# A hybrid layer whose context columns and preparation run within the feed-forward part before it

## The chip, the cores and the metric

The kernel runs on one core of one Trainium2 chip. The metric is the device time of one execution in microseconds (us). TensorE (PE in the profile) multiplies, and its weight loads (PEld) run beside; VectorE (DVE), ScalarE (ACT) and GpSimd (POOL) work element by element; SyncE (SP) issues nearly all DMAs. Each engine takes its instructions in the order written in its own stream, and waits for the others by semaphores.

## The reference

The program is two blocks. The first has layers of feed-forward, mixer, feed-forward on 256 tokens of width 1024; its last part is called FFN(1,1) here. The second works on 256 latent tokens (the output of the first) and 256 context tokens (an input of the program) and begins with the hybrid layer, cut to what matters here:

```
p_lat, p_ctx = norm(h) @ w_in, norm(ctx) @ w_in       # 1792 RWKV columns, then 1536 of attention
rc = rwkv_prepare(p_ctx[:, :1792]);  rl = rwkv_prepare(p_lat[:, :1792])
yc, sf, sb = wkv_bidir(rc, zero state)                # both directions
yl, _, _   = wkv_bidir(rl, (sf, sb))                  # begins from the context's last states
a_lat, a_ctx = rwkv_output(yl, rl), rwkv_output(yc, rc)
o_l = differential attention of latents over latents and context
o_c = differential attention of the context over itself
out = [a, norm(o)] @ w_out                            # for latents and context
```

The context's half, `p_ctx` and `rc`, needs nothing of the first block. `yl` needs `sf` and `sb`, so the two `wkv_bidir` are serial.

## The kernel before

Everything is float32. A weight tile is loaded by SP (`wr`, `wload`), cast to a high part by ACT (`wh`) and a low part is subtracted by DVE (`wl`; while `poolw` is 3, every third one by POOL); a product is then three matmuls (`mm3`, lines 135 to 137). A framework takes the order in which the code is written, priorities (`rank`, `beside`) and the life of the buffers in pools, simulates the engines, and from that fixes each engine's stream.

`ffn` runs over eleven tiles j of 256 hidden columns: an up-projection into PSUM banks B, the gate on ACT and DVE, a down-projection into banks A, which are kept over all j. Its argument `side(j)` is called once per j and may insert other work. Before, `side(3)` normalises the context and transposes it (`norm_T`). After FFN(1,1) comes `hybrid`, stage by stage:

- the latents' norm, then seven units of 256 RWKV columns for the context (`cols(0, u)`: 48 matmuls of 256 wide each, 336 in all; `mix` then adds the two neighbours in time);
- `rw_prep` for the context (gates, decays, and a serial triangular inverse on DVE, here called the Neumann loop: 62 operations at L1162), and beside it the attention's columns for both token sets (288 matmuls of 512 wide, `A<-xH,wh` and `A<-wh,xH`);
- the context's attention, `attention(0)`, among the latents' 336 column matmuls (`cols(1, u)`); the latents' mixed columns go to DRAM (`lr`);
- `chains` for the context: eight groups of heads and directions over four chunks, a recurrence in which each hop is a few small matmuls with copies on ACT and DVE between (L1355, L1363, L1368, L1373, L1379, L1389), and whose preparation (`s`, `Z` on POOL, `W`, `sys` on DVE, L1322) can go ahead. Beside it runs `rw_prep` for the latents, from the `lr` read back;
- `chains` for the latents, with `attention(1)` beside it;
- the output projection, then the next part (`mlp2`).

Buffers live in pools on a left and a right side of SBUF that close in order, so a pool's place decides when the next stage's loads may start.

## Time and profile before

| | us |
|---|---|
| median of 3 runs | 3198.22 (3195.32 to 3206.99) |
| profiled execution | 3196.53 |
| its span | 3194.8 |
| FFN(1,1) | 1467 to 1663 |
| latents' norm, context's RWKV columns | 1663 to 1713 |
| `rw_prep` of the context, attention columns | 1713 to 1797.5 |
| `attention(0)`, latents' RWKV columns | 1797.5 to 1858 |
| context's chains, `rw_prep` of the latents | 1858 to 2026 |
| latents' chains, `attention(1)` | 2026 to 2158 |
| output projection | 2158 to 2224 |

The span runs from the first instruction to the last; 1.7 us of the execution lie around it. The stages are read from where the lines of each begin and end on TensorE; the last Neumann operation of the latents falls at 2030.8. The profile's granted clock (PEclk) is TensorE's, in parts of 2.4 GHz: 0.959 over the span. In a row of windows there stand the stretch and its length, then the busy time and, in brackets, the count of instructions of PE, PEld, DVE, ACT and POOL, the granted clock, the DMA engines' busy share and GB/s. A row of a group has line, engine, operation, what is written and read, the count, busy us in all, mean ns of one, and the idle time just before them with what ended it.

### The profile page before, as it was taken

The numbers are of one execution on the slowest core, as the hardware profiler recorded it, in microseconds if no ns is written. First come the engines' busy times: TensorE is split into PE (matmuls) and PEld (weight loads), VectorE is DVE, ScalarE is ACT, GpSimd is POOL, SyncE is SP. The second block draws the span as 40 slices with busy tenths as digits, with TensorE's granted clock in tenths as the row PEclk, the third lists the DMA queues.
The fourth block names the chain that finished last, engine by engine and source line by source line (L and its number), as shares of the span: only waits on it lengthen the run. The fifth ranks groups of instructions, "written<-read, shape, count | busy, mean of one in ns | idle before, by whom it ended". The sixth has DMA issues, their size and how long they took to land.

```text
span 3194.8 us, 42767 instructions
## 1 busy us (share of the span) xinstructions
PE 2955.0 (92%) x15184; PEld 2459.9 (77%) x15184; DVE 2202.2 (69%) x3572; ACT 1589.6 (50%) x2907; POOL 608.2 (19%) x806
## 2 busy tenths in 40 slices
PE   8999989889989998999999978898999989998898
PEld 7877878668778787877887867786777777777787
DVE  6666875676677668657565767886766548999755
ACT  5454544545455454445446575665423325565444
POOL 1221020121221003001012155430110002444100
PEclk9999999899999999999999987898999989999999
DMA  7666655556667654647544611115466424344564
GB/s 248 217 208 179 177 161 171 172 189 209 202 199 224 181 168 131 203 145 244 176 142 146 191 45 41 51 41 191 147 192 190 152 74 114 111 116 126 185 186 139
DMA packets 383577, 509.76 MB, mean 160 GB/s; under 512 B 39938, under 2 KB 245140, under 8 KB 382980
## 3 DMA queue, kind: packets, MB, share of 16 engines
q1 hardware_dynamic: 383364, 507.03, 51.6%
q8 instruction: 120, 1.97, 0.3%
q14 instruction: 93, 0.76, 0.1%
HBM read 494.07 MB, written 12.88 MB: 159 GB/s over the span
## 4 chain that ended last, share of the span: by engine, by line
PE 59%; DVE 17%; DMA 8%; issue 7%; ACT 5%; POOL 3%; SPq 0%; DVEq 0%; ACTq 0%; POOLq 0%
PE A L135 11%; PE A L137 11%; PE A L136 11%; DMA wr<-in_ada_w_dram 5%; PE B L136 5%; PE B L135 5%; PE B L137 5%; DVE wl L253 4%; DVE scv L1476 2%; ACT wh L252 2%; DVE adacc L706 2%; PE T L243 1%; DMA wr<-in_mlp_w_dram 1%; PE F L135 1%; PE F L137 1%
## 5 line engine op out<-in xcount | busy, mean ns | idle before, releaser
L253 DVE TENSOR_TENSOR wl<-wr,wh 128x1024 fp32r<-128x1024 f32 x720 | 902.0, 1258 | 481.8 <-ACT wh L252 448.0
L252 ACT CAST wh<-wr 128x1024 fp32r<-128x1024 f32 x720 | 751.5, 1049 | 712.4 <-PE A L137 320.7
L135 PE MATMUL B<-wh,xH 128*128 128x512 f32 x832 | 330.4, 403 | 7.4 <-ACT xH L252 5.5
L136 PE MATMUL B<-wl,xH 128*128 128x512 f32 x832 | 332.3, 400 | 3.1 <-DVE wl L253 3.0
L137 PE MATMUL B<-wh,xL 128*128 128x512 f32 x832 | 330.2, 397 | 0.0
L135 PE MATMUL A<-xH,wh 128*128 128x256 f32 (+1 forms) x960 | 305.8, 321 | 1.7 <-ACT zm L950 1.0
L706 DVE SCALAR_TENSOR_TENSOR adacc<-wr,silu_c,adacc 128x512 f32<-128x512 f32 x232 | 181.6, 801 | 177.3 <-DMA wr<-in_ada_w_dram 104.5
L136 PE MATMUL A<-xL,wh 128*128 128x256 f32 (+1 forms) x960 | 303.7, 318 | 0.0
L137 PE MATMUL A<-xH,wl 128*128 128x256 f32 (+1 forms) x960 | 298.1, 318 | 1.4 <-DVE wl L253 0.8
L136 PE MATMUL A<-wl,hTH 128*128 128x512 f32 x736 | 285.9, 391 | 3.1 <-DVE wl L253 3.1
L135 PE MATMUL A<-wh,hTH 128*128 128x512 f32 x736 | 282.9, 391 | 4.6 <-ACT hTH L252 3.1
L137 PE MATMUL A<-wh,hTL 128*128 128x512 f32 x736 | 282.0, 392 | 0.1
L136 PE MATMUL A<-wl,xH 128*128 128x512 f32 x544 | 217.6, 400 | 9.2 <-DVE wl L253 6.3
L135 PE MATMUL A<-wh,xH 128*128 128x512 f32 x544 | 215.7, 404 | 4.9 <-ACT xH L255 3.6
L137 PE MATMUL A<-wh,xL 128*128 128x512 f32 x544 | 217.1, 400 | 0.0
L135 PEld LDWEIGHTS A<-xH,wh 128*128 128x128 f32 x960 | 184.3, 192 | 14.2 <-issue 1.9
L137 PEld LDWEIGHTS A<-xH,wl 128*128 128x128 f32 x960 | 181.8, 192 | 14.9 <-issue 1.9
L136 PEld LDWEIGHTS A<-xL,wh 128*128 128x128 f32 x960 | 184.3, 192 | 11.4 <-issue 1.5
L135 PEld LDWEIGHTS B<-wh,xH 128*128 128x128 f32 x832 | 159.1, 192 | 42.5 <-ACT xH L252 7.2
L136 PEld LDWEIGHTS B<-wl,xH 128*128 128x128 f32 x832 | 159.3, 191 | 37.6 <-DVE wl L253 6.5
L137 PEld LDWEIGHTS B<-wh,xL 128*128 128x128 f32 x832 | 159.4, 192 | 33.1 <-DVE xL L253 0.4
L205 POOL TENSOR_TENSOR ms<-ss 128x1 f32<-128x1 f32 x44 | 16.1, 367 | 875.1 <-ACT jk L268 451.0
(530 smaller groups left out, 6153.0 us busy)
## 6 DMA issues: line engine op xcount, KB each, us to landing
wr<-in_w_ffn_gu_dram SPq DMA_DIRECT2D x352, 256.0 KB
wr<-in_w_in_dram SPq DMA_DIRECT2D x144, 512.0 KB
wr<-in_mlp_w_dram SPq DMA_DIRECT2D x128, 512.0 KB
wr<-in_ada_w_dram SPq DMA_DIRECT2D x96, 512.0 KB
wr<-in_w_ffn_down_dram SPq DMA_DIRECT2D x88, 512.0 KB
wr<-in_w_branch_dram SPq DMA_DIRECT2D x48, 512.0 KB
wr<-in_ssd_w_in_dram SPq DMA_DIRECT2D x48, 512.0 KB
wr<-in_hy_w_in_dram SPq DMA_DIRECT2D x40, 512.0 KB
```

Source lines behind the costliest of these rows:

```text
L135: mm(acc, xH, wH, start=start, stop=False)
L136: mm(acc, xH, wL, start=False, stop=False)
L137: mm(acc, xL, wH, start=False, stop=stop)
L205: nc.gpsimd.tensor_tensor(out=m, in0=ss[:, 0:1], in1=ss[:, 1:2], op=ALU.add)
L243: nc.tensor.transpose(pt[:, i * P : (i + 1) * P], src[:, i * P : (i + 1) * P], self.ident)
L252: nc.scalar.copy(H, src)
L253: nc.vector.tensor_tensor(out=L, in0=src, in1=H.bitcast(F32), op=ALU.subtract)
L706: nc.vector.scalar_tensor_tensor(out=a, in0=w[:, k % 2, :], scalar=c, in1=a, op0=ALU.mult, op1=ALU.add)
L1476: nc.vector.scalar_tensor_tensor(out=v3(y), in0=z[:, :, j : j + S], scalar=self.scw(j, f), in1=v3(y), op0=ALU.mult, op1=ALU.add)
```

## The change

- `hybrid_open` is called before FFN(1,1): the hybrid layer's parameters are loaded there.
- `hybrid_ctx` is a generator that `side(j)` steps through, by the table `SIDE` (2, 3, 4, ... steps for each j): context norm, the seven units of columns (now in the order `RWU`, each unit in one PSUM bank F, operands swapped, so that the product comes out transposed), then all of `rw_prep`.
- After FFN(1,1) the layer has three stretches: the context's chains with the latents' RWKV columns stepped among them (one step every two rounds of the chains; `poolw` is 3); then `rw_prep` of the latents and, at the same rank, the attention's columns and after them `attention(0)`; then the latents' chains with `attention(1)`, as before.
- The normalised tokens of both sets go through DRAM (`xs`) to the stretch of the attention's columns; the round trip of `lr` is gone. `rw_prep` runs its large products on DVE alone (before, for the latents some were on POOL).
- Chains' buffers `nch` are 8 in the first stretch and 9 in the last, `s2` 2 or 3 (before 9 and 3). The feed-forward part's last down weights come from the common pool (`own=False`). Sides of pools change (`swap`), and the output projection's inputs `x` are loaded earlier in SP's stream, before the last chains.

```diff
+RWU = (2, 3, 6, 0, 1, 4, 5)
+SIDE = (2, 3, 4, 4, 4, 4, 5, 5, 5, 5, 5, 0)
...
-    def ffn(self, l, i, h, side=None, g_in=None):
+    def ffn(self, l, i, h, side=None, g_in=None, own=True):
...
+    def rw_cols(self, u, xT):
+        nc, pr, W = self.nc, self.pr, self.I["hy_w_in_2"][0]
+        ws = [self.wload([W[q * 512 : q * 512 + 512, u * 256 : u * 256 + 256]], 4) for q in range(2)]
+        ps = self.accTF() if self.two else self.accF()
+        for i in range(2):
+            fs = slice(i * P, i * P + P)
+            for k in range(KT):
+                wh, wl = (a[:, k % 4, fs] for a in ws[k // 4])
+                self.mm3(ps[:, i * S : i * S + S], wh, wl, xT[0][:, k, :], xT[1][:, k, :], k == 0, k == KT - 1)
+            if i == 0:
+                yield 1
...
+    def hybrid_ctx(self):
...
+        for u in RWU:
+            yield from self.rw_cols(u, xT)
+            yield 1
+        self.v0 = self.rv
+        yield from self.rw_prep(self.bgs[0], itertools.repeat(self.accF), nc.vector, nc.vector)
...
-        self.norm_mod(self.lat_mods, [h[:, t, :] for t in range(NT)], xT, 2)
+        xT = tuple(Halves([self.t(self.rwp, (P, 4, S), "tmp", F32R, 4) for _ in range(2)]) for _ in range(2))
+        self.norm_mod(self.lat_mods, [h[:, t, :] for t in range(NT)], xT)
...
-        for u in range(7):
-            cols(0, u)
-        cx = self.rw_prep(pt, pa, rk, v[0], gd[0], bg[0], itertools.cycle((self.accB, self.accB, self.accF)), nc.vector, nc.vector)
-        self.poolw = 3
+        pl, self.nch = self.pool(ec, "rwc", "right"), 8
+        cg = self.chains(pl, self.arrs, self.v0, y[0], None, True)
+        self.poolw = 3
...
+        for n in itertools.count():
+            if next(cg, None) is None:
+                break
+            if n == 1:
+                lg = lat()
+            if n >= 2 and n % 2 == 0:
+                next(lg, None)
...
+        for _ in self.rw_prep(bg[1], itertools.cycle((self.accB, self.accB, self.accF)), nc.vector, nc.vector):
+            pass
         with self.rank(r0):
...
-        for u in range(7):
-            cols(1, u)
-            for _ in range(3):
-                next(dg, None)
+            el.close()
+            for _ in attention(0):
+                pass
+            ed.close()
...
-        for _ in self.chains(pl, cx, v[0], y[0], None, True):
-            pass
-        with self.rank(r0):
-            nc.sync.dma_start(out=rk, in_=lr)
-            lx = self.rw_prep(pt, self.pool(el, "rwl", "right"), rk, v[1], gd[1], bg[1], itertools.repeat(self.accF), nc.vector, nc.gpsimd)
...
         def side(j):
-            if j == 3:
...
+            for _ in range(SIDE[j]):
+                next(cg, None)
-        self.ffn(1, 1, h, side)
+        self.ffn(1, 1, h, side, own=False)
```

How instructions move, at three places. First VectorE's stream at the end of FFN(1,1) of the kernel before (L275 is the residual, L233 and L235 the latents' norm, L253 a split of a weight):

```order
L275 SCALAR_TENSOR_TENSOR h_81<-xn_14642,rs_14651,h_81 128x512
L275 SCALAR_TENSOR_TENSOR h_81<-xn_14646,rs_14651,h_81 128x512
L253 TENSOR_TENSOR wl_14871<-wr_14868,wh_14870 128x1024
L233 SCALAR_TENSOR_TENSOR xn_14673<-h_81,rs_14671,md_13571 128x512
L233 SCALAR_TENSOR_TENSOR xn_14683<-h_81,rs_14671,md_13571 128x512
L235 TENSOR_TENSOR xn_14673<-xn_14673,md_13569 128x512
L253 TENSOR_TENSOR wl_14901<-wr_14898,wh_14900 128x1024
L235 TENSOR_TENSOR xn_14683<-xn_14683,md_13569 128x512
L233 SCALAR_TENSOR_TENSOR xn_14703<-h_81,rs_14701,md_13571 128x512
L233 SCALAR_TENSOR_TENSOR xn_14713<-h_81,rs_14701,md_13571 128x512
```

The same place after (L294 is the residual, L252 and L254 the latents' norm, L1211 on `tmp` the Neumann loop of the context, L272 on `tmp` the low halves of the transposed latents, L1361 the chains' preparation):

```order
L294 SCALAR_TENSOR_TENSOR h_84<-xn_15488,rs_15497,h_84 128x512
L294 SCALAR_TENSOR_TENSOR h_84<-xn_15492,rs_15497,h_84 128x512
L1211 TENSOR_TENSOR tmp_15055<-tmp_15055,tmp_15056 128x31
L1211 TENSOR_TENSOR tmp_15056<-tmp_15054,tmp_15055 128x30x2
L1211 TENSOR_TENSOR tmp_15055<-tmp_15055,tmp_15056 128x30x2
```

```order
L1211 TENSOR_TENSOR tmp_15055<-tmp_15055,tmp_15056 128x2x30
L1211 TENSOR_TENSOR tmp_15056<-tmp_15054,tmp_15055 128x31
L1211 TENSOR_TENSOR tmp_15055<-tmp_15055,tmp_15056 128x31
L272 TENSOR_TENSOR tmp_15507<-F_15522,tmp_15505 128x4x128
L272 TENSOR_TENSOR tmp_15507<-F_15552,tmp_15505 128x4x128
L272 TENSOR_TENSOR tmp_15508<-T_15532,tmp_15506 128x4x128
L1466 COPY vr_15616<-v_13417 128x512
L272 TENSOR_TENSOR tmp_15508<-T_15562,tmp_15506 128x4x128
L1361 TENSOR_TENSOR sys_15608<-B_15603,c_hyb_13004 128x2x128
```

Before, the norm follows the residual at once, and the Neumann loop stands a stage later. Now all 62 of its operations stand between the residual and the four low halves, without which no latent column can be multiplied.

Second TensorE's stream in the context's chains of the kernel before (`F<-ari,bk` is `rw_prep` of the latents, the rest are the chains):

```order
L1389 MATMUL A_17390<-c_all_67,E_17120 128x128
L1379 MATMUL A_17394<-xv_3449_16842,sys_17133 128x64 x2
L1373 MATMUL A_17416<-u_3598_17316,Z_17192 128x128
L1239 MATMUL F_18441<-ari_3908_18314,bk_3910_18316 64x64 x16
L1379 MATMUL A_17420<-xv_3449_16842,sys_17075 128x64 x2
L1379 MATMUL A_17442<-xv_3458_16878,sys_17097 128x64 x2
L1373 MATMUL A_17464<-u_3602_17326,Z_17156 128x128
L1368 MATMUL A_17468<-u_3619_17381,sys_17239 128x128
```

And after (L154 to L156 on F are the latents' columns, L1381, L1382, L1414 and L1469 the chains):

```order
L156 MATMUL F_15737<-tmp_15505,wl_15728 128x256
L154 MATMUL F_15737<-tmp_15505,wh_15727 128x256
L155 MATMUL F_15737<-tmp_15507,wh_15727 128x256
L1414 MATMUL A_15657<-xv_3178_15579,W_15607 128x64 x2
L1469 MATMUL T_15590<-c_all_67,v_13417 128x128 x4
L156 MATMUL F_15737<-tmp_15505,wl_15728 128x256
L154 MATMUL F_15737<-tmp_15505,wh_15727 128x256
L155 MATMUL F_15737<-tmp_15507,wh_15727 128x256
L156 MATMUL F_15737<-tmp_15505,wl_15728 128x256
```

The chains' matmuls now stand in the same stream between runs of 7 to 12 column matmuls; the last column matmul stands where 13 of the chains' 32 hops are done, and the other 19 have only the beginning of `rw_prep` beside them.

Third TensorE's stream at `attention(0)` of the kernel before (L1122, L1134 and L1139 are the attention, L135 to L137 the latents' columns):

```order
L1139 MATMUL F_16305<-dv_16031,dwT_16303 128x128 x2
L1122 MATMUL B_16446<-dk_16030,qz_3290_16114 128x256
L1134 MATMUL T_16329<-c_all_67,dw_16316 128x128 x2
L137 MATMUL A_16686<-xH_12994,wl_16690 128x256
L135 MATMUL A_16686<-xH_12994,wh_16689 128x256
L136 MATMUL A_16686<-xL_12995,wh_16689 128x256
```

And after (L1169, L1181 and L1186 are the attention, L154 to L156 the last of the attention's columns, L1331 the end of `rw_prep`):

```order
L154 MATMUL A_18137<-wh_18230,xH_17850 128x512
L155 MATMUL A_18137<-wl_18231,xH_17850 128x512
L156 MATMUL A_18137<-wh_18230,xL_17851 128x512
L1169 MATMUL B_18289<-dk_18275,qz_3817_18280 128x256
L1169 MATMUL B_18296<-dk_18275,qz_3817_18280 128x256
L1169 MATMUL B_18316<-dk_18275,qz_3817_18280 128x256
L1169 MATMUL B_18323<-dk_18275,qz_3817_18280 128x256
L1181 MATMUL T_18306<-c_all_67,dw_18293 128x128 x2
L1169 MATMUL B_18345<-dk_18275,qz_3818_18281 128x256
L1186 MATMUL F_18311<-dv_18276,dwT_18309 128x128 x2
```

Before, column matmuls stand between the attention's steps. Now the attention stands alone, from the last column matmul to the first matmul of the latents' chains 25 rows on; on VectorE its operations stand behind the latents' Neumann loop, and ahead of the latents' chains.

## Rows read from the trace of the kernel before

**Rows 1.** Page: TensorE's busy share, and the granted clock in 40 slices.

```profile
PE 2955.0 (92%) x15184; PEld 2459.9 (77%) x15184; DVE 2202.2 (69%) x3572; ACT 1589.6 (50%) x2907; POOL 608.2 (19%) x806
...
PEclk9999999899999999999999987898999989999999
```

**Rows 2.** Windows by stage: us, busy (count) by engine, PEclk, DMA share, GB/s.

```profile
1467.00:1663.00 196.00, 193.29 (x871) 157.08 (x872) 116.90 (x154) 90.49 (x133) 6.77 (x19) 0.99 0.54 173
1663.00:1713.00 50.00, 44.43 (x337) 42.60 (x335) 31.53 (x52) 33.25 (x60) 15.02 (x26) 0.93 0.56 171
1713.00:1797.50 84.50, 84.15 (x477) 64.73 (x477) 46.00 (x49) 42.10 (x71) 13.10 (x8) 1.00 0.51 145
1797.50:1858.00 60.50, 55.21 (x425) 52.88 (x424) 57.55 (x166) 40.44 (x113) 12.85 (x16) 1.00 0.54 168
1858.00:2026.00 168.00, 135.00 (x836) 111.01 (x834) 123.28 (x343) 94.84 (x327) 84.05 (x125) 0.78 0.13 39
2026.00:2158.00 132.00, 117.74 (x831) 105.13 (x832) 106.60 (x356) 91.31 (x362) 60.76 (x100) 0.94 0.16 49
2158.00:2224.00 66.00, 56.30 (x223) 42.38 (x224) 42.25 (x62) 35.38 (x46) 2.84 (x6) 0.90 0.54 188
```

**Rows 3.** Windows: context columns (256 wide), feed-forward matmuls (512 wide).

```profile
1689.00:1704.00 15.00, 15.00 (x127) 15.00 (x127) 9.02 (x10) 12.16 (x23) 3.21 (x5) 1.00 0.69 200
1500.00:1600.00 100.00, 99.62 (x452) 81.81 (x451) 57.14 (x70) 45.06 (x58) 0.00 (x0) 1.00 0.61 189
```

**Rows 4.** Groups of VectorE, 1797.5 to 1858: count, busy, mean ns, idle.

```profile
L1162 DVE TENSOR_TENSOR tmp<-tmp,tmp 128x31 f32<-128x31 f32 (+15 forms) x62 | 23.9, 386 | 6.6 <-DMA tmp<-in_id_dram 6.0
L1124 DVE TENSOR_REDUCE dmx<-B 128x1 f32<-128x256 f32 x16 | 6.6, 413 | 0.0
L1131 DVE SCALAR_TENSOR_TENSOR dw<-dw,dmx,dw 128x256 f32<-128x256 f32 x8 | 4.2, 524 | 0.0
L1130 DVE TENSOR_SCALAR dw<-dw,dmx 128x256 f32<-128x256 f32 x8 | 2.7, 342 | 0.0
L1128 DVE RECIPROCAL dmx<-dmx 128x1 f32<-128x1 f32 x16 | 2.5, 156 | 0.3 <-ACT dw L1127 0.2
```

**Rows 5.** Groups of VectorE, 1663 to 1689.

```profile
L233 DVE SCALAR_TENSOR_TENSOR xn<-h,rs,md 128x512 f32<-128x512 f32 x4 | 2.8, 747 | 0.4 <-POOL rs L209 0.4
L235 DVE TENSOR_TENSOR xn<-xn,md 128x512 f32<-128x512 f32 x4 | 2.7, 685 | 0.0
L275 DVE SCALAR_TENSOR_TENSOR h<-xn,rs,h 128x512 f32<-128x512 f32 x3 | 2.2, 749 | 0.1
L253 DVE TENSOR_TENSOR xL<-T,xH 128x512 fp32r<-128x512 f32 x2 | 1.4, 684 | 0.0
```

**Rows 6.** Windows at the start of the context columns.

```profile
1680.00:1685.00 5.00, 2.98 (x13) 2.84 (x14) 1.80 (x10) 1.44 (x4) 0.70 (x2) 0.58 0.29 77
1685.00:1690.00 5.00, 5.00 (x34) 5.00 (x33) 2.36 (x7) 1.99 (x5) 0.57 (x2) 0.74 0.73 209
```

**Rows 7.** Windows: context's chains, latents' chains, first hop to last.

```profile
1880.70:2026.00 145.30, 123.72 (x797) 102.98 (x796) 115.64 (x323) 78.53 (x281) 70.27 (x89) 0.81 0.10 30
2044.20:2158.00 113.80, 106.70 (x787) 96.50 (x787) 93.21 (x317) 75.25 (x308) 48.90 (x80) 0.99 0.10 32
```

**Rows 8.** Groups of TensorE, 2026 to 2158, attention(1) among the chains.

```profile
L1122 PE MATMUL F<-kr,qr 128*128 128x256 f32 x32 | 11.4, 440 | 1.6 <-DVE kr L1112 1.0 <-ACT dw L1127 0.4
L1122 PE MATMUL F<-dk,qz 128*128 128x256 f32 x32 | 10.5, 413 | 0.0
```

**Rows 9.** Chain of waits, 1850 to 1885: start us, us, what.

```profile
1853.69 2.62 DMA db<-tmp
...
1858.59 5.82 DMA rk<-lr
```

**Rows 10.** Chain of waits, 2155 to 2182.

```profile
2157.52 8.38 DMA on<-od
...
2178.25 0.85 PE A L135 x2
```

More of the change, by code (lines that the diff above doesn't have):

```diff
@@ L292, in do_down @@
                 for j in js:
-                    own = dict(pool=p, bufs=(2, 2, 2)) if j == NJ - 1 else {}
-                    ws.append([self.wload([wd[j * 256 : j * 256 + 256, n * 512 : n * 512 + 512]], **own) for n in range(2)])
+                    mine = dict(pool=p, bufs=(2, 2, 2)) if own and j == NJ - 1 else {}
+                    ws.append([self.wload([wd[j * 256 : j * 256 + 256, n * 512 : n * 512 + 512]], **mine) for n in range(2)])
                 for t in range(NT):
@@ new lines, in hybrid_open, with rw_in @@
+        self.bgs = [scr((P, 8, S), f"bg{s}") for s in range(2)]
+        self.rwa, self.rwp = self.pool(self.ea, "rwa", "right"), self.pool(self.et, "rwp", "right")
+        self.hybrid_setup(b)
+    def rw_in(self):
+        b = self.hyb
+        self.rk, self.rv, self.gd = self.t(b, (P, 9, S), "rk"), self.t(b, (P, 4, S), "v"), self.t(b, (P, S), "gd")
+    def rw_cols(self, u, xT):
[9 more added lines that the diff above has]
+                yield 1
+        z = self.t(self.rwp, (P, 2, 514), "kk" if u % 2 else "kb")
+        nc.gpsimd.memset(z[:, :, 0:1], 0.0)
+        nc.gpsimd.memset(z[:, :, S + 1 : S + 2], 0.0)
+        pv = ps.rearrange("p (i s) -> p i s", i=2)
+        nc.scalar.copy(z[:, :, 1 : S + 1], pv)
+        n = z[:, :, S + 2 : 2 * S + 2]
+        nc.gpsimd.tensor_tensor(out=n, in0=z[:, :, 0:S], in1=z[:, :, 2 : S + 2], op=ALU.add)
+        for i in range(2):
+            f = 2 * u + i
+            o = self.rv[:, f - 8, :] if 8 <= f < 12 else self.gd if f == 13 else self.rk[:, min(f, 8), :]
+            nc.scalar.activation(o, pv[:, i, :], AF.Identity, scale=pr["mu1"](f))
+            nc.vector.scalar_tensor_tensor(out=o, in0=n[:, i, :], scalar=pr["mu2"](f), in1=o, op0=ALU.mult, op1=ALU.add)
@@ L923, in hybrid @@
+        xT = tuple(Halves([self.t(self.rwp, (P, 4, S), "tmp", F32R, 4) for _ in range(2)]) for _ in range(2))
+        self.norm_mod(self.lat_mods, [h[:, t, :] for t in range(NT)], xT)
+        for i in range(2):
+            for k in range(0, KT, 4):
+                nc.sync.dma_start(out=self.xs[i][:, k : k + 4, S : 2 * S], in_=xT[i][:, k : k + 4, :].bitcast(F32))
         for e in eh:
             e.close()
-        b = self.pool(eb, "hyb")
-        self.pad(b, 32)
-        self.hybrid_setup(b)
@@ L973, in hybrid @@
         with self.rank(r0):
             DQ = 1792
+            px = self.pool(el, "hyx")
+            xT = self.xT(px, "x", n=2 * S)
+            for k in range(0, KT, 2):
+                for i in range(2):
+                    nc.sync.dma_start(out=xT[i][:, k : k + 2, :].bitcast(F32), in_=self.xs[i][:, k : k + 2, :])
             qks, vds = scr((P, 8, 2, S), "qks"), scr((P, 4, 512), "vds")
@@ L1021, in hybrid, with attention @@
-        for e in (ec, et, ea):
-            e.close()
-        y.append(self.t(self.pool(et, "hyy"), (P, 4, S), "y1"))
-        pl = self.pool(ec, "rwc")
-        dg = attention(1, None)
-        cg = self.chains(pl, lx, v[1], y[1], self.Sfin, False)
+            self.poolw = 0
+            def attention(s):
+                pd = self.pool(ed, "dif")
+                if s:
+                    self.load_consts(pd, "dif")
+                ns = 1 + s
+                q, k, v = self.t(pd, (P, 4, S), "dq"), self.t(pd, (P, 4, ns, S), "dk"), self.t(pd, (P, 2 * ns, 512), "dv")
+                nc.sync.dma_start(out=q, in_=qks[:, 0:4, s])
+                for i in range(ns):
+                    nc.sync.dma_start(out=k[:, :, i], in_=qks[:, 4:8, i])
+                nc.sync.dma_start(out=v, in_=vds[:, 0 : 2 * ns, :])
+                return self.diff(s, q, [k[:, :, i] for i in range(ns)], v, od, pd)
@@ L1029, in hybrid @@
+            el.close()
+            for _ in attention(0):
+                pass
+            ed.close()
+        self.et.close()
+        es.close()
+        xs = [self.t(self.pool(e, "x"), (P, NT, D), "x") for e in exs]
+        y.append(self.t(b, (P, 4, S), "y1"))
+        pl, self.nch = self.pool(ec, "rwc", "right"), 9
+        dg = attention(1)
+        cg = self.chains(pl, self.arrs, self.rv, y[1], self.Sfin, False)
         for n in itertools.count():
@@ L1155, in diff, with rw_prep @@
             nc.sync.dma_start(out=od[:, 2 * s + t, :], in_=o)
-    def rw_prep(self, pt, pa, rk, v, gd, bg, first, inv, alt):
+    def rw_prep(self, bg, first, inv, alt):
         nc, pr, I = self.nc, self.pr, self.I
+        pt, pa, rk, v, gd = self.rwp, self.rwa, self.rk, self.rv, self.gd
         C, NC = 64, S // 64
```

185 lines of the change are left out of this document (81 added, 104 removed).

## The prediction

> **What bounds the kernel now.** I read the page first: TensorE is busy 92% of the span, so most stages are bound by its stream, and the granted clock has one low place in the middle [rows 1]. Then the windows by stage [rows 2]. FFN(1,1), the attention columns and the latents' columns have TensorE busy for 193.3 of 196, 84.2 of 84.5 and 55.2 of 60.5 us at a clock of 0.99 to 1.00: work that is taken out of them shortens them one for one, and work put into them lengthens them so, as long as it is matmuls. The context's chains are another kind: 168 us with TensorE busy 135.0 at a clock of 0.78, VectorE 123.3, ScalarE 94.8, GpSimd 84.1. No engine is full; the recurrence is a string of short matmuls and copies that wait for each other. The latents' chains, with the attention beside them instead of `rw_prep`, take 132.
>
> Everything up to FFN(1,1) and from `mlp2` on keeps its order on every engine, so the whole effect lies between the start of FFN(1,1) and the end of the output projection. The quantity I follow is the time from the end of FFN(1,1), 1663, to the last hop of the latents' chains, 2158: 495 us, plus what FFN(1,1) grows.
>
> **The change part by part.** The same matmuls run after as before. What changes is which of them stand beside work that leaves TensorE idle.
>
> *FFN(1,1) grows.* It takes in 336 column matmuls of 256 wide. The stretch that holds nothing else did 127 in 15.00 us, 0.118 us each [rows 3], so 39.7 us. It takes in `rw_prep` of the context. Its share of TensorE is read from the stage that held it: 84.15 us, less 288 matmuls of 512 wide at 0.227 (100 us of the feed-forward part did 452 matmuls of which 28 are short transposes [rows 3]: between 0.220 and 0.235), 65.4, less some 21 columns at 0.118, 2.5: about 16 us. As TensorE has 2.7 us of idle in the 196, none of this hides: 39.7 + 16 = 56. Beside it, VectorE's and ScalarE's loads grow by at most what the two stages that held these steps had, 31.5 + 46.0 and 33.3 + 42.1 [rows 2]: to 194 and 166 of 256. Both fit, but each takes its stream in order, and the large operations of `rw_prep` will now and then keep a weight split waiting; two loads of ScalarE's tables are added. I add 4 us: FFN(1,1) is 60 us longer, between 56 (nothing stalls) and 73 (each of some dozen operations of `rw_prep` costs TensorE about 1.2 us, as long as its larger ones last).
>
> *A gap opens at the end of FFN(1,1).* Before, the latents' norm stood a stage away from any matmul that needed it; now the first latent columns wait for it, and there is no other matmul to run. On VectorE, in its order: the rest of the residual (four operations of 0.749, 2.9 with a part of the sums), the norm (four of 0.747 and four of 0.685, 5.7), the low halves (four of 0.684, 2.7) [rows 5], and the Neumann loop between them, 62 operations, 23.9 us [rows 4]. With some 2 us for the small statistics it is 37 us in which TensorE has nothing but a few transposes. It is no less than 32, if the residual and the norm overlap with ScalarE as well as they can, and 45 if the loop begins late, because its input, which goes through DRAM, leaves TensorE only some 7 us before the feed-forward part ends (a transfer of that kind took 2.6 and one back 5.8 [rows 9]). The chains can begin about 9 us after the gap, as the loop's result goes through DRAM too.
>
> *Context's chains with the latents' columns.* No stage of before holds this pair. The bounds are the two stretches of chains, from first hop to last: 113.8 us with the attention beside them, 145.3 with `rw_prep` [rows 7]. The columns are 336 × 0.118 = 39.7 us of TensorE. The attention of the faster stretch had 21.9 in its largest two groups [rows 8] and more in smaller ones, so for TensorE the columns are not far from the attention. On VectorE they are lighter than either: the stage that held them had 57.6 [rows 2], of which 23.9 were a Neumann loop and 16.0 the attention [rows 4], which leaves 17.7. Against that stands that in the order the columns run ahead, at 13 hops of 32, so that the later hops run nearly alone at the pace of their own waits. I take the middle of the two rows, 130, and 9 for the start and 4 for the prologue: 143, range 115 to 165.
>
> The clock is a part of that range. At the start of the context columns, where TensorE was busy for 2.98 of 5 us, the granted clock was 0.58, and 0.74 in the next 5 us although it was busy for all of them [rows 6]: much of that at the lower of its two levels, 1.2 GHz; and the context's chains had 0.81 over their hops against 0.99 for the latents' [rows 7]. The Trainium skill, TensorE: Matmul & The Clock Gate, section "HAM oscillation — how this bites in real kernels", says that waits between groups of matmuls drop the array to half its clock, so that each group begins cold. It speaks against this change, which makes a gap of 37 us and sets thin chains behind it; the trace agrees with it here. By the rule the last hops would stay cold, and the sum would be by the upper bound instead of the middle.
>
> *`rw_prep` of the latents and the attention's columns, then `attention(0)`.* The columns are 65.4 us, the part of `rw_prep` on TensorE that isn't done beside the chains some 11: 76. On VectorE the Neumann loop, 23.9, and the 46.0 of the stage that held the context's `rw_prep` and the same columns, 70 in all [rows 2, 4], are covered by them. `attention(0)` isn't covered any more: on VectorE its largest groups sum to 16.0 [rows 4], with the small ones 21 us, in one string of steps through three engines, and its input goes through DRAM: 30, between 21 and 40. Together 106, range 95 to 118.
>
> *Latents' chains.* From the last Neumann operation, 2030.8, to the end, 2158, before: 127. The trip through DRAM of that loop, 2.6 + 5.8 [rows 9], is now long over when they begin: 121, range 115 to 128.
>
> *Output projection.* Its first matmul stands at 2178.3, 20 us after the last hop; a load of 8.4 us that started at the last hop ended late among the others [rows 10]. Two of the others, `x`, now go ahead. I take 3 us off, between 0 and 6.
>
> Sum: 60 + 37 + 143 + 106 + 121 = 467 against 495, so 28 less, and 3 from the projection: 31 less. Against the profiled execution's 3196.5 that is 3165.5; the median of the runs is 1.7 above that execution. I say 3165.
>
> **The rivals.**
>
> *A: the chains are overloaded.* One mechanism at one place: the columns stand in TensorE's stream between the hops, 7 to 12 at a time, and each hop waits behind such a run. At the full clock a run is about 1.2 us, at the lower level 2.4. If the stretch goes at the pace of the slower row, 145.3, and the columns come on top of it, it is 145 + 40 + 13 = 198 in place of 143: 55 more, 3220. It decides from 190 on, where the sum is slower than before by over 0.5%. For it speaks that the slower stretch's clock was low all the time; against it that in the latents' chains as much TensorE work was hidden in 113.8.
>
> *B: the clock rule of the skill's page.* The gap and the thin hops behind it keep the clock down without the columns adding to it: the stretch goes as before, 145 + 9 + 4 = 158, and the gap is 42: 20 more, 3185. For it speaks the row of 0.81; against it that the stage with columns among attention's steps kept 1.00 [rows 2].
>
> *C: the context's chains go like the latents'.* The stretch is 114 + 9 + 4 = 127, and the overhang of `attention(0)` 24 in place of 30: 22 less than the sum, 3143. For it speaks that VectorE has less beside the chains than in both rows.
>
> *D: the feed-forward part doesn't take it.* Its weight splits wait behind `rw_prep`'s operations on VectorE: 73 in place of 60, 3178.
>
> **How the numbers follow.** My forecast 0.40, C 0.22, D 0.12, B 0.14, A 0.12. The widths of the terms, taken as independent (8, 6, 25, 12, 6, 3), combine to about 30 us around 3165. The range reaches from a little under C to between B and A: 3122 to 3206. Half a per cent, 16 us, is about what a measurement of this kernel can tell from no change. Faster than 3182: my forecast, C, D and a little of B, less what their widths carry over the line, 0.66. Slower than 3214: most of A and a little of B, 0.12. Between: 0.22. My forecast's own range is 3150 to 3180.
>
> **What would show it.** FFN(1,1) from 1467 ending near 1723, with TensorE over 97% busy and no idle of more than 2 us. Then about 37 us with nearly no matmul, and VectorE busy with the 62 operations. The granted clock after it below 1 for the first few us, above 0.85 over the chains. The chains' first hop near 1770, the last near 1903; the last column matmul well before it. Then 76 us of full TensorE, 25 to 35 us of thin work on the attention, and the latents' chains ending near 2130. The prediction is wrong if the chains of the context last over 165 us or the feed-forward part grows by over 75, if the gap is not there, or if the attention is not exposed.

## The result, and the profile after

The changed kernel takes 3237.81 us (median of 4, 3235.05 to 3238.30) against 3196.91 of before: ratio 1.0119, 95% interval 1.0098 to 1.0141. It is slower by some 38 to 41 us where 31 less were forecast. Its profiled execution has a span of 3233.3 us, 38.5 more than that of before.

The page's two lines that answer to [rows 1]:

```profile
PE 2955.5 (91%) x15184; PEld 2449.5 (76%) x15184; DVE 2196.1 (68%) x3573; ACT 1593.9 (49%) x2895; POOL 605.5 (19%) x815
...
PEclk9999999899999999999997979899999999999999
```

No engine has more work than before by more than 5 us; what grew is waiting. Windows of the changed kernel by the stretches of the prediction (columns as in [rows 2]): feed-forward part, gap, context's chains with the latents' columns, attention's columns, a wait, `attention(0)`, the start of the latents' chains, these chains, the output projection:

```profile
1470.00:1738.00 268.00, 259.81 (x1375) 210.45 (x1376) 172.71 (x224) 144.63 (x220) 23.57 (x37) 0.97 0.60 184
1738.00:1775.30 37.30, 4.97 (x19) 2.99 (x17) 33.34 (x79) 7.85 (x18) 7.33 (x14) 0.57 0.33 111
1775.30:1943.60 168.30, 153.22 (x1060) 136.58 (x1060) 108.04 (x305) 115.54 (x352) 85.08 (x133) 0.85 0.23 65
1943.60:2025.30 81.70, 80.99 (x403) 62.64 (x402) 40.42 (x84) 20.43 (x30) 7.33 (x4) 0.97 0.43 136
2025.30:2039.80 14.50, 0.00 (x1) 0.03 (x1) 0.00 (x0) 1.95 (x5) 0.83 (x2) 0.66 1.01 338
2039.80:2063.50 23.70, 17.61 (x84) 12.48 (x84) 18.10 (x76) 16.73 (x66) 1.24 (x2) 0.92 0.20 26
2063.50:2081.60 18.10, 9.64 (x40) 8.10 (x39) 7.56 (x19) 16.78 (x58) 13.31 (x24) 0.53 0.58 192
2081.60:2198.10 116.50, 106.98 (x795) 96.95 (x794) 96.94 (x329) 76.44 (x307) 51.15 (x82) 1.00 0.05 12
2198.10:2263.50 65.40, 57.41 (x226) 42.10 (x225) 41.88 (x62) 34.86 (x46) 2.81 (x6) 0.92 0.55 191
```

| term | forecast | measured | where |
|---|---|---|---|
| feed-forward part, later end | 60 | 74.9 | 1663 to 1737.9 |
| gap | 37 | 37.4 | to 1775.3 |
| context's chains, latents' columns | 143 | 168.3 | to 1943.6 |
| attention's columns, `attention(0)` | 106 | 119.9 | to 2063.5 |
| latents' chains | 121 | 134.6 | to 2198.1 |
| sum against 495 | -28 | +40 | |
| output projection | -3 | -1 | 66.3 to 65.3 us |

Four terms of five are too small. The largest miss, 25 us, is at the end of the context's chains. The next windows are, row by row: the start of the context's chains, with the latents' columns beside them; the columns' rest; the middle of the context's chains; their end, in which the last ten of 32 hops finish; for comparison, the end of the latents' chains, in which the last seventeen finish; and, after the dots, a piece of the fourth row:

```profile
1775.30:1795.00 19.70, 17.19 (x113) 16.55 (x114) 9.77 (x21) 14.48 (x41) 14.34 (x34) 0.77 0.60 161
1795.00:1856.00 61.00, 61.00 (x532) 61.00 (x531) 38.69 (x104) 44.63 (x141) 46.57 (x62) 1.00 0.33 96
1856.00:1900.00 44.00, 38.87 (x286) 34.56 (x284) 30.50 (x109) 28.68 (x116) 23.57 (x38) 0.96 0.08 25
1900.00:1943.60 43.60, 36.16 (x137) 24.46 (x136) 29.08 (x74) 27.75 (x55) 0.60 (x1) 0.58 0.07 18
2157.00:2198.10 41.10, 37.78 (x280) 33.73 (x279) 34.67 (x126) 21.73 (x89) 7.25 (x12) 1.00 0.12 33
...
1915.00:1930.00 15.00, 15.00 (x48) 10.51 (x46) 10.92 (x23) 7.18 (x17) 0.00 (x0) 0.50 0.01 1
```

From 1900 on TensorE does half as many matmuls as the latents' chains in nearly the same time, at a granted clock of 0.58. Among the last hops stand 30 of the 32 products of `rw_prep` for the latents (L1247, 64 rows high). In the order they come there because they take PSUM banks B, which the chains' own preparation holds until then.

VectorE takes part in it too. From 1927.2 to 1934.4 it does six large operations of `rw_prep` in a row and none of the chains. TensorE stands still for 4.82 us up to 1935.0, waiting for an operation of ScalarE that itself waited for the last of the six (timeline: start, us, what, and in brackets the idle time before it with what ended it):

```profile
1929.51 2.44 DVE L1211 TENSOR_TENSOR big<-kb,tmp 64x1024 f32<-64x1024 f32 x2
1934.98 1.22 PE L1247 MATMUL F<-rk,lup 64*128 64x256 f32 x2 [4.82 <-ACT tmp L1248]
```

Three of the six, the two of this row and one of 1.20 us, ran on GpSimd in the kernel before.

The 14.5 us without a matmul are read from the chain of waits, 2010 to 2045 (start, us, what; SPq is SyncE's issuing):

```profile
2025.68 0.39 SPq L1092
2026.15 0.45 SPq L1049
2026.69 0.38 SPq L1313
2027.13 0.63 SPq L1091
2027.81 0.55 SPq L1092
2028.46 0.54 SPq L1059
2029.05 10.62 DMA dk<-qks
```

L1091 and L1092 are the loads of `x`, which I had credited with 3 us: their buffers come free with the last attention column, so they leave just ahead of the attention's own load, which lands 10.62 us later on full DMA engines (1.01 in the window above).

### The profile page after: what moved, and what is told of

Read it like the earlier page. It is cut to its first block, busy times and chain, and to the rows that moved or that the text cites. A ratio compares the mean times of both kernels' runs of the same rounds, so it can differ in the third digit from the quotient of the medians.

```text
span 3233.3 us, 42712 instructions
## 1 busy us (share of the span) xinstructions
PE 2955.5 (91%) x15184; PEld 2449.5 (76%) x15184; DVE 2196.1 (68%) x3573; ACT 1593.9 (49%) x2895; POOL 605.5 (19%) x815
## 4 chain that ended last, share of the span: by engine, by line
PE 62%; DVE 15%; DMA 8%; issue 6%; ACT 5%; POOL 3%; SPq 0%; DVEq 0%; ACTq 0%; POOLq 0%
PE A L154 11%; PE A L156 11%; PE A L155 11%; DMA wr<-in_ada_w_dram 5%; PE B L155 5%; PE B L156 5%; PE B L154 5%; DVE wl L272 3%; DVE scv L1535 2%; ACT wh L271 2%; DVE adacc L725 2%; PE F L154 1%; PE F L155 1%; PE T L262 1%; PE F L156 1%
## 5 line engine op out<-in xcount | busy, mean ns | idle before, releaser
L272 DVE TENSOR_TENSOR wl<-wr,wh 128x1024 fp32r<-128x1024 f32 x715 | 897.2, 1261 | 499.8 <-ACT wh L271 490.8
L154 PE MATMUL B<-wh,xH 128*128 128x512 f32 x832 | 331.6, 404 | 7.1 <-ACT xH L271 5.7
L156 PE MATMUL B<-wh,xL 128*128 128x512 f32 x832 | 331.2, 399 | 0.0
L154 PE MATMUL A<-wh,hTH 128*128 128x512 f32 x736 | 284.5, 394 | 5.4 <-ACT hTH L271 3.1
L156 PE MATMUL A<-wh,hTL 128*128 128x512 f32 x736 | 284.0, 393 | 0.1
L154 PE MATMUL A<-xH,wh 128*128 128x256 f32 (+1 forms) x736 | 240.7, 330 | 1.5 <-ACT k L681 0.7
L156 PE MATMUL A<-xH,wl 128*128 128x256 f32 (+1 forms) x736 | 237.2, 326 | 1.7 <-DVE wl L272 1.5
L155 PE MATMUL A<-xL,wh 128*128 128x256 f32 (+1 forms) x736 | 238.6, 325 | 0.0
L154 PE MATMUL A<-wh,xH 128*128 128x512 f32 x544 | 215.5, 403 | 4.8 <-ACT xH L274 3.5
L156 PE MATMUL A<-wh,xL 128*128 128x512 f32 x544 | 216.0, 398 | 0.0
L154 PEld LDWEIGHTS B<-wh,xH 128*128 128x128 f32 x832 | 158.9, 192 | 41.6 <-ACT xH L271 7.0
L156 PEld LDWEIGHTS B<-wh,xL 128*128 128x128 f32 x832 | 159.3, 191 | 33.8 <-issue 1.2
L154 PEld LDWEIGHTS A<-wh,hTH 128*128 128x128 f32 x736 | 138.5, 189 | 37.2 <-ACT hTH L271 4.2
L155 PEld LDWEIGHTS A<-wl,hTH 128*128 128x128 f32 x736 | 138.8, 189 | 35.9 <-DVE wl L272 6.2
L736 POOL TENSOR_TENSOR adal<-adacc,adah 128x512 fp32r<-128x512 f32 x40 | 76.7, 1917 | 460.1 <-ACT adah L735 413.4
L156 PEld LDWEIGHTS A<-wh,hTL 128*128 128x128 f32 x736 | 139.0, 189 | 30.2 <-DVE hTL L272 0.8
```

The source lines that it names most:

```text
L154: mm(acc, xH, wH, start=start, stop=False)
L155: mm(acc, xH, wL, start=False, stop=False)
L156: mm(acc, xL, wH, start=False, stop=stop)
L272: nc.vector.tensor_tensor(out=L, in0=src, in1=H.bitcast(F32), op=ALU.subtract)
L736: nc.gpsimd.tensor_tensor(out=al, in0=a, in1=ah.bitcast(F32), op=ALU.subtract)
```

## The experiments

Changes are to the changed kernel unless said otherwise. Ratios are to the kernel before, measured together with each, and are to be held against 1.0119 (1.0098 to 1.0141).

**The loads of `x` late.**

```diff
-        xs = [self.t(self.pool(e, "x"), (P, NT, D), "x") for e in exs]      # before the latents' chains
+        xs = [self.t(self.pool(e, "x"), (P, NT, D), "x") for e in exs]      # after them
```

> One part undone: the buffers of x (the output projection's inputs) are taken after the latents' chains again, so their four loads stand behind the attention's loads in SyncE's stream. Theory (the changed kernel's 14.5 us without a matmul from 2025.3 to 2039.8 come from SyncE: the loads of x wait there for the last attention column, whose buffers they take over, and the attention's loads are queued behind them): the stretch before attention(0) shrinks to about 5 us, the output projection gives back 2 to 6 us, so 3225 to 3231 against 3237.8. Rival (the attention's own load is slow, 10.6 us from issue to landing, whatever stands ahead): 3236 to 3244, with the idle time still above 12 us.

3237.27 us, ratio 1.0133 (1.0117 to 1.0148). Its wait before `attention(0)`, and the time from the last hop to the output projection's first weight matmul:

```profile
2028.30:2037.00 8.70, 0.00 (x0) 0.00 (x0) 0.00 (x0) 2.04 (x5) 0.82 (x2) 0.65 1.01 334
2194.90:2216.80 21.90, 9.96 (x22) 3.71 (x20) 9.57 (x18) 15.60 (x19) 0.00 (x0) 0.73 1.02 408
```

Theory and rival are each half right. The loads cost 5.8 of the 14.5 us; the other 8.7 are the trip of the attention's inputs itself. And what is won there is lost behind: the projection begins 21.9 us after the last hop instead of 14.3.

**The context's work earlier.**

```diff
-SIDE = (2, 3, 4, 4, 4, 4, 5, 5, 5, 5, 5, 0)
+SIDE = (4, 6, 7, 7, 7, 7, 8, 8, 8, 0, 0, 0)
```

> One table changed: SIDE takes more steps per tile, so the context's work comes earlier within the feed-forward part, and 24 of the 62 Neumann operations stand ahead of the residual. Theory (the gap of 37 us after the feed-forward part is VectorE's string of residual, norm and Neumann loop, and its length goes on the path): the gap shrinks by 9 to 12 us, and the kernel takes 3225 to 3231. Rival (the latent columns that start earlier only run into the chains, which start when the Neumann result is back, or the feed-forward part grows by what the gap loses): 3235 to 3242.

3236.26 us, ratio 1.0126 (1.0110 to 1.0143): no difference that can be told.

```profile
1469.70:1741.40 271.70, 259.29 (x1376) 208.70 (x1376) 176.85 (x243) 144.98 (x221) 21.54 (x36) 0.98 0.59 185
1741.40:1770.00 28.60, 3.15 (x13) 2.15 (x12) 25.63 (x56) 6.78 (x15) 7.48 (x10) 0.57 0.26 92
```

The gap falls from 37.4 to 28.6 us, nearly as the theory had it. But from its first matmul to its last the feed-forward part takes 271.7 us instead of 265.9 (1472.0 to 1737.9), which takes back two thirds, and the first hop of the context's chains comes 323 us after that first matmul in both kernels. So both halves of the rival are seen.

**The context's work out of the feed-forward part** (`SIDE` all zeros).

> The change's main part undone alone: SIDE is all zeros, so the context's norm, columns and rw_prep run between the feed-forward part and the chains, with the latents' norm beside. Theory (the feed-forward part is bound by TensorE and hides none of the 336 columns and of rw_prep's matmuls, but it does hide rw_prep's string of steps on ScalarE and VectorE): the feed-forward part falls back from 268 to about 196 us, the stretch to the first chain hop grows from 37 to 150 to 170 us, 3285 to 3300 in all. Rival (it hides nothing, the steps would be as short outside): 3230 to 3250.

3309.19 us, ratio 1.0358 (1.0337 to 1.0379).

```profile
1473.00:1663.70 190.70, 189.68 (x848) 154.73 (x848) 111.82 (x144) 89.17 (x123) 3.85 (x10) 0.99 0.61 193
1663.70:1844.10 180.40, 96.63 (x540) 72.65 (x540) 92.32 (x156) 66.22 (x114) 24.18 (x38) 0.64 0.29 88
```

The theory holds, with a longer string than estimated: the feed-forward part falls by 75 us, and the stretch to the first latent column grows from 37 to 180. The stretch grows by 68 us more than the feed-forward part falls: what the move hides is not the matmuls but the waiting between them, and the lower clock (0.64 over that stretch).

**Other PSUM banks for `rw_prep` of the latents.**

```diff
-self.rw_prep(bg[1], itertools.cycle((self.accB, self.accB, self.accF)), nc.vector, nc.vector)
+self.rw_prep(bg[1], itertools.cycle((self.accT1, self.accF)), nc.vector, nc.vector)
```

> One resource changed: rw_prep of the latents takes the PSUM banks T and F for its first products instead of B, B and F, so that it need not wait for the chains' preparation, which fills both B banks until three chain hops before the end. Theory (the context's chains end late because rw_prep's 32 products fall together behind the last hops, 40 us for the last three of 32 at a granted clock of 0.50): the products spread over the hops from 1857 on, the last three hops take 13 to 20 us, the chains end near 1920 instead of 1943, and the kernel takes 3212 to 3222. Rival (the chains' end is set by their own string of steps and the columns before, and rw_prep only moves to where it slows other hops): 3232 to 3245.

3252.85 us, ratio 1.0174 (1.0153 to 1.0196): slower still. Context's chains after the last latent column:

```profile
1856.00:1885.00 29.00, 26.07 (x119) 18.95 (x118) 12.63 (x36) 24.81 (x72) 10.64 (x16) 0.74 0.13 37
1885.00:1915.00 30.00, 29.73 (x132) 24.87 (x132) 17.32 (x53) 15.45 (x50) 14.15 (x17) 0.57 0.00 1
1915.00:1945.00 30.00, 23.90 (x124) 18.37 (x124) 24.84 (x63) 8.81 (x30) 4.99 (x8) 0.66 0.00 1
```

The last hops became quick, and those before them slow: the chains end at 1959.6. The rival was right that the products slow whatever hops they stand beside, though the kernel is 8 us above its range; the low clock goes where the products go. The expectation's 40 us for the last three hops are in the trace 39 us for the last eight.

**A gate: `rw_prep` only after the chains.**

```diff
         ec.close()
+        for k, c in ((4, 0), (8, 192)):
+            o = self.rk[:, k, :].rearrange("p (a b) -> p a b", a=4)
+            nc.vector.scalar_tensor_tensor(out=o, in0=y[0][:, :, c : c + 64], scalar=0.0, in1=o, op0=ALU.mult, op1=ALU.add)
```

Two small VectorE operations add zero times the chains' output to inputs of `rw_prep`, which so has to wait for it.

> Two small VectorE operations added (0 times the chains' output, added to parts of the latents' mixed columns), so that rw_prep of the latents can't begin before the context's chains have ended. Theory (rw_prep's products and activations stand between the last hops, at a granted clock of 0.58 over those 44 us, and cost the chains some 26 us, where the latents' chains do their last eight hops in 13): the last eight hops take 13 to 18 us instead of 39 and the context's chains end at 1915 to 1922 instead of 1943.6. rw_prep then runs beside the attention's columns; as its string of steps is longer than these (133 us before, from 1717 to 1850, with its loop), the loop ends 20 to 30 us after the last column, and the kernel takes 3222 to 3240. Rival (the chains end late by themselves, after the columns delayed them): they end at 1935 or later, and the kernel takes 3245 to 3265.

3220.48 us, ratio 1.0076 (1.0061 to 1.0091): clear of the changed kernel. End of the chains, then the attention's columns, then the wait for the attention's load:

```profile
1885.00:1918.00 33.00, 27.34 (x184) 24.51 (x183) 23.79 (x93) 12.63 (x56) 6.20 (x11) 0.88 0.06 18
1918.00:2009.30 91.30, 91.17 (x461) 65.24 (x462) 47.67 (x78) 44.63 (x67) 7.24 (x4) 0.97 0.37 120
2009.30:2024.00 14.70, 0.90 (x6) 0.48 (x4) 9.53 (x29) 2.91 (x7) 0.88 (x2) 0.61 1.02 321
```

The chains end at 1917.9, 25.7 us earlier, and the attention's columns take 91 us instead of 82 with `rw_prep` beside them. The theory holds for the chains; the loop ends 10 us behind the last column, not 20 to 30, and the kernel is 1.5 us under the range. The gate takes away `rw_prep` as a whole: what its products, the low clock and VectorE's string each cost, it does not tell, and `rw_prep` with part of its operations on GpSimd again was not tried.

The context's chains with the latents' columns alone beside them take 123.8 us from first hop to last (1794.1 to 1917.9), against 116.5 of the latents' chains with `attention(1)`. That does not make the columns free: in the first kernel of the next experiment the latents' chains, with only `attention(0)` beside them, take 100.8 us. As far as the two sets of chains can be compared, the columns, some 40 us of matmuls, then cost 23 us more than that lighter neighbour. No run has whole chains with nothing beside them.

**`attention(0)` among the latents' chains**, stepped ahead of `attention(1)`, first at every third round, with and without the gate; then at every second and every round with the gate; then with the earlier `SIDE`.

```diff
-            for _ in attention(0):
-                pass
-            ed.close()
...
+        def both():
+            yield from attention(0)
+            ed.close()
+            yield from attention(1)
```

> attention(0) is stepped among the latents' chains, ahead of attention(1), instead of alone between the attention's columns and these chains. Theory (its 24 us, its load and the chains' start behind it are exposed: 38 us from the last column to its end and 18 to the chains' first hop): the first hop of the latents' chains comes at 2040 to 2048 instead of 2081.6, the chains take 10 to 18 us longer than 116, and the kernel takes 3210 to 3222. Rival (TensorE is busy 107 of 116.5 us in those chains already, so attention(0) costs there nearly what it cost alone): 3228 to 3242.

> Both: rw_prep of the latents begins only after the context's chains, and attention(0) is stepped among the latents' chains. Theory (the two costs are apart): context's chains end at 1915 to 1922, the attention's columns near 2000, the loop near 2025, the latents' chains' first hop near 2038 with the attention beside them: 3200 to 3215. Rival (rw_prep after the chains is the longest string and sets the latents' chains' start, so the gate takes back what it gives): the same as with attention(0) moved alone, within 4 us, or slower.

> The gate on rw_prep as before, and attention(0) and attention(1) are stepped together at every second round of the latents' chains (with every third, attention(1) fell behind the chains and ran alone for 116 us). Theory: the chains' first hop at about 2030, the chains with both attentions 125 to 135 us, little of the attention left behind them: 3195 to 3207. Rival (attention(1) still trails the chains): 3215 to 3240.

> The same, with the attentions stepped at every round, so that both are done before the chains' last hops. Theory: TensorE is nearly full over 130 to 140 us from 2030 on, nothing trails: 3195 to 3207. Rival (the attention, ahead of the hops in the streams, now slows the chains by more than it took alone): 3210 to 3225.

> As the first of these, with SIDE taking more steps early. Theory (the earlier Neumann loop gave 2 to 4 us where it was changed alone): 2 to 4 us less than the first. Rival (the longer feed-forward part takes that back): within 1 us of it.

In this order 3283.57, 3263.11, 3251.45, 3250.98 and 3252.51 us, ratios 1.0275, 1.0214, 1.0173, 1.0177 and 1.0177, each to within 0.0023. All are slower than the changed kernel. In the first four the times lie outside both sides of the expectations; in the last the rival holds, the earlier `SIDE` changes nothing (1.1 us). In the first the chains begin at 2050.4 and end at 2151.2, 47 us earlier, but `attention(1)` comes behind them alone (first two rows); at every round the chains themselves take 183 us (third row, of that kernel):

```profile
2050.00:2151.20 101.20, 93.66 (x685) 85.18 (x683) 80.59 (x301) 67.21 (x295) 45.43 (x79) 0.95 0.03 8
2151.20:2267.00 115.80, 70.81 (x207) 45.64 (x206) 49.71 (x121) 43.04 (x94) 8.18 (x12) 0.62 0.27 96
```

```profile
2033.00:2215.70 182.70, 137.79 (x880) 115.41 (x881) 117.88 (x409) 96.67 (x381) 54.60 (x91) 0.89 0.17 57
```

Two attentions one after the other share one set of buffers, and their strings don't fit beside one set of chains. It is not TensorE that is full there (137.79 of 182.70 us); which wait stretches the chains was not tried.

**Attention's columns in two halves**, context's tokens first, `attention(0)` stepped among the second half; each weight tile is loaded and split twice. Alone and with the gate:

```diff
+            for s in range(2):
+                for u in range(4):
+                    accs = self.tform(xTs[s], lambda a, c: [W[a:c, DQ + u * 256 : DQ + u * 256 + 256]], self.accA)
...
+                    for _ in range(2):
+                        next(dg, None)
...
+                if s == 0:
+                    e0.close()
+                    dg = attention(0)
```

> The attention's columns are computed in two halves, first the context's tokens, then the latents' (each weight tile loaded and split twice), and attention(0), which needs the first half alone, is stepped among the second. Theory (14.5 us of waiting for its load and 23.7 of attention(0) lie open on the path): no idle stretch above 5 us between the context's chains and the last column, that stretch grows from 78.5 to 88 to 100 us, and the latents' chains' first hop comes at 2050 to 2062 instead of 2081.6: 3208 to 3222. Rival (the loop of rw_prep ends only 15 us before attention(0) begins on VectorE and sets the chains instead, or the doubled splits delay the columns): 3228 to 3245.

> The same with the gate on rw_prep. Theory (the tail of the context's chains and the open attention(0) are two separate costs of the change; the first is 17 us in the kernel's time when measured alone, the second 20 to 30): chains end at 1918, columns near 2022, first hop of the latents' chains near 2040: 3190 to 3204, no slower than the kernel before by more than 0.3%. Rival (rw_prep, begun late, has its loop behind the last column, and what one gains the other loses): 3206 to 3222.

3226.35 us, ratio 1.0095 (1.0075 to 1.0115), which overlaps that of the changed kernel; with the gate 3206.56, ratio 1.0028 (1.0017 to 1.0039). Without the gate, then with it, from the chains' end to the last column and from there or from `attention(0)`'s end to the latents' first hop:

```profile
1946.20:2046.00 99.80, 95.55 (x648) 86.17 (x648) 69.42 (x148) 44.80 (x97) 19.09 (x9) 0.92 0.70 208
...
2054.10:2076.80 22.70, 10.83 (x38) 8.17 (x39) 9.85 (x24) 16.13 (x57) 14.72 (x26) 0.51 0.46 154
```

```profile
1917.70:2029.30 111.60, 107.68 (x724) 90.10 (x725) 81.77 (x166) 72.14 (x147) 19.50 (x9) 0.94 0.58 179
2029.30:2054.20 24.90, 13.63 (x62) 11.33 (x60) 15.11 (x48) 18.95 (x70) 13.59 (x23) 0.66 1.00 287
```

The attention is covered, but only some 12 to 14 us come of it, not 20 to 30: with the gate, the way from the context's chains' end to the latents' first hop is 136.5 us against 149.2 without the split. Alone, the split brings the first hop to 2076.8, where the theory had 2050 to 2062, and its time lies between theory and rival; with the gate the time is the rival's, and the loop does end behind the last column (2037.4, column 2029.3). Both repairs together bring back about three quarters of the loss.

**What holds the latents' chains' start.** On top of both repairs: `attention(0)` ranked behind `rw_prep`; the same with `x` late; the same with the earlier `SIDE`.

```diff
+                    with self.rank(r1):       # r1: the priority at the end of rw_prep
+                        for _ in range(2):
+                            next(dg, None)
```

> Split columns and gate, and attention(0) ranked behind the rest of rw_prep, so that VectorE takes the Neumann loop's operations first where both are ready. Theory (the loop, spread among attention(0)'s operations until 2037, sets the chains' start): the loop ends 4 to 10 us earlier, and so does the chains' first hop: 3197 to 3203. Rival (the loop begins late since rw_prep does, and each of its operations waits for the one before, so the order beside it matters little): 3204 to 3209.

> The same with the buffers of x taken after the latents' chains, so that 2 MB of loads no longer stand between the last column and the loop's result. Theory (they delay the loop's result and attention(1)'s inputs): first hop 4 to 8 us earlier, of which the output projection takes 5 to 8 back: within 3 us of the kernel with x early. Rival (nothing waits for them there): first hop the same, 4 to 8 us slower.

> The first of these with SIDE taking more steps early: 1 to 3 us less than it if the gap after the feed-forward part is partly on the path, as when changed alone (1.5 less); no difference within 1 us otherwise.

3202.87 (1.0025, 1.0013 to 1.0038), 3212.53 (1.0054, 1.0034 to 1.0075) and 3204.17 us (1.0030, 1.0019 to 1.0040). In the first the loop's last operation comes at 2033.0 instead of 2037.4, and the first hop at 2055.5 instead of 2054.2. So the loop's end does not set the chains' start: that the first time lies within the theory's range is luck, and it can't be told from the 1.0028 without the rank. With `x` late the first hop is no earlier either (2061.8), and the kernel is slower by more than the rival's 8 us. The earlier `SIDE` makes no difference in the time, though in its profiled execution the first hop comes 8.4 us earlier (2047.1): what follows the last hop took 11 us longer there. The first kernel from the loop's end to the first hop:

```profile
2033.00:2055.50 22.50, 9.73 (x39) 7.76 (x39) 11.51 (x27) 16.42 (x60) 14.78 (x26) 0.62 0.82 261
```

ScalarE is the busiest engine there, as in the changed kernel (16.78 of 18.1). But the trace of the changed kernel shows a second string. The first matmuls of `attention(1)` stand ahead of the first hop in TensorE's order, and wait there for their load, 5.5 us in all (timeline, the third row is the first hop):

```profile
2074.86 1.19 PE L1149 MATMUL F<-dq,c_dif 128*128 128x256 f32 x2 [3.96 <-DMA dq<-qks]
2077.63 1.19 PE L1149 MATMUL F<-dk,c_dif 128*128 128x256 f32 x2 [1.58 <-DMA dk<-qks]
2081.57 0.44 PE L1422 MATMUL A<-E,Z 128*128 128x128 f32 x2
```

ScalarE had that hop's operand `E` ready at 2076.1, before this load was in. With `x` late on top of both repairs the load is in at 2038.7, and TensorE waits for ScalarE instead (3.73 us at one place). So the traces show both strings ahead of the start, now one and now the other ending last; neither was tried by itself.

No version beats the kernel before; the best, with split, gate and rank, is slower than it by 0.25%.

## Why the prediction was wrong

*What bounds the kernel* was right: matmuls moved into the feed-forward part lengthened it one for one.

*The feed-forward part grows by 60*: it is 72 us longer (268 for 196) and ends 74.9 later, 3 of them from a later start. Between the two kernels' windows TensorE has 66.5 us more busy, where 56 were forecast, and 5.5 more idle, where 4 were. Most of the miss is the price of the matmuls: the 336 columns took 45.7 us there instead of 39.7, and `rw_prep`'s products 20.6 instead of 16. TensorE's waits in the changed kernel, beside the one at its start:

```profile
PE F L154 <- ACT rk L960: 2.6, 1, 2.6
PE F L1325 <- ACT at L1296: 2.0, 1, 2.0
PE F L1247 <- ACT tmp L1248: 1.4, 2, 0.9
```

They are waits for the one bank F, which the columns and `rw_prep` share. The term was mis-sized by 12, just within its bound of 73. Rival D came near this size, but it put the time on waits for VectorE's splits, and these were 0.4 us.

*The gap of 37* was right to 0.4 us. What it is worth was not tested alone, since the earlier `SIDE` moved the feed-forward part as well.

*Context's chains, 143*: this is the step that failed. For the pair of chains and columns the number is right: with `rw_prep` gated off the stretch takes 144.5 us (1773.4 to 1917.9). In part that is luck, for the way to the first hop took 20.7 us where 13 were forecast, and the hops 123.8 where 130 were. But the prediction let the later hops "run nearly alone at the pace of their own waits", and the account of the order ahead of it saw only the beginning of `rw_prep` beside them. In fact 30 of the 32 products stand among the last ten hops, with their activations and VectorE's large operations; the last eight hops took 39 us there where they take 15 with the gate. Rival A named the right stretch and the wrong mechanism: with the columns alone beside them the chains kept to 144.5, not 198. Rival C, by which the stretch goes like the latents' chains at 127, did not come about with the gate either.

*The clock.* The granted clock over the hops was 1.00 among the columns and 0.58 among `rw_prep`'s products; with the gate the last hops, alone, had 0.88. The Trainium skill, TensorE: Matmul & The Clock Gate, section "HAM oscillation — how this bites in real kernels", puts the lower clock down to waits between groups of matmuls. The gap of this case agrees with it (0.57 in it, 0.77 in the 20 us after). The tail agrees only in part: from 1900 to 1915 TensorE waits a little (12.81 of 15 us busy, 0.74), but between 1915 and 1930 the rows show it busy for all of 15 us at 0.50, the lower of the two levels, so with no gap that the profile shows. Rival B, by which the gap itself would keep the hops cold, is refuted: the hops that follow the gap ran at 1.00.

*Attention's columns and `attention(0)`, 106*: 119.9. The columns took 81.7 for 76, `attention(0)` with its load 38.2 for 30, within its bound of 40. What I had not seen is the queue: the loads of `x` wait on SyncE for the last attention column and stand ahead of the attention's load. I had priced their move at the output projection alone.

*Latents' chains, 121*: 18.1 to the first hop and 116.5 over the hops. The hops were right (113.8 before). The step that failed is that the loop's trip through DRAM would be saved (and by its own rows that would have made it 118.8, 127.2 less 8.4, not 121): the chains' start is not held by it. In the kernel before, too, ScalarE was the busiest engine from the loop's end to the first hop (11.47 of 13.40 us), and TensorE's last wait there was for it:

```profile
2030.80:2044.20 13.40, 9.93 (x44) 8.26 (x45) 9.06 (x25) 11.47 (x42) 10.46 (x19) 0.69 0.36 83
...
2043.96 0.43 PE L1355 MATMUL A<-xv,W 128*128 128x64 f32 x2 [1.94 <-ACT xv L1414]
```

Of ScalarE's 16.78 us before the first hop of the changed kernel most are copies that build the chains' operands:

```profile
L1390 ACT COPY W<-big 64x128 f32<-64x128 f32 x20 | 5.9, 296 | 0.2
L1473 ACT COPY xv<-T 64x256 f32<-64x256 f32 x12 | 4.4, 366 | 0.3
L1405 ACT COPY xv<-Sfin 64x64 f32<-64x64 f32 x16 | 3.9, 243 | 0.3
```

Before, this prologue ran while the loop and its trip did (the first hop 13.4 us after the loop); now it begins when `attention(0)` is done.

So the mechanism of the gain was there, in part: the chains took the latents' columns in an attention's place for 7 us more. But three strings came to lie open: `rw_prep` at the chains' end, `attention(0)` with its load, and the chains' own start.

## What to carry to other kernels

When work moves, follow in the order not only the piece that moves but also what then falls beside the neighbour's last steps: a string of dependent steps can cost the chain that it stands beside more than a run of independent matmuls does. Here the 32 products of `rw_prep`, 11.6 us of TensorE in the feed-forward part, cost the chains some 25 us with what hangs on them; the 336 columns, some 40 us of TensorE, cost them 7 us more than `attention(1)` did and 23 more than `attention(0)`. Price a load that goes earlier in its queue by what stands behind it there, not only by who waits for it. And a stage that is removed takes its cover with it: list the strings that ran under it, since each wants a new place.

## What was not expected of the hardware

TensorE was granted 0.50 and 0.57 of its clock in stretches in which the profile has it busy for 15.00 of 15 us (above) or 29.73 of 30 (the kernel with other banks, 1885 to 1915), both with `rw_prep`'s 64-row products among short hops; among the 128-row columns and the same hops it had 1.00. Which of the two, rows or spacing, decides was not tried.
